# Two products of four units drawn forward, their five others in interleaved pairs, in place of one unit of eight products (Griffin-style decoder block, one Trainium2 core)

## The chip, the core and the metric

The kernel is one program on one core of a Trainium2 chip. The metric is device time in microseconds, as the median of several runs. Five engines matter, each with its own queue, which it works off in the order in which the kernel was written: TensorE (PE, with its weight loads PEld), VectorE (DVE), ScalarE (ACT), GpSimd (POOL) and SyncE (SP, which here only issues DMAs). Where one engine needs another's result it waits at that place, with everything behind it in its queue.

## The reference, cut to what matters

```python
h = rms_norm(x, norm_g)                          # x: 1 x 2048 x 1024, float32
u = jnp.einsum('bsd,dc->bsc', h, w_in)           # 1024 -> 8704 columns
v_c, b_c, c_c, z_c, q, k, v, z_a, gate_logits = jnp.split(u, SPLIT_POINTS, axis=-1)
y_c = b_c * causal_depthwise_conv(c_c * v_c, conv_w)
y_c = y_c * jax.nn.silu(z_c)
y_a = jnp.einsum('bsc,cd->bsd', y_c, w_conv_out)
q = rms_norm(q.reshape(b, s, 16, 64), q_norm_g)
k = rms_norm(k.reshape(b, s, 4, 64), k_norm_g)
o = sliding_window_attention(q, k, v, sinks) * jax.nn.silu(z_a)     # window 128
y_b = jnp.einsum('bsc,cd->bsd', o, w_attn_out)
g_a, g_b = jnp.split(jax.nn.sigmoid(gate_logits + gate_b), 2, axis=-1)
out = x + jnp.einsum('bsd,de->bse', g_a * y_a + g_b * y_b, w_out)
```

All that the change touches is in the second line: the columns q (1024 of them, in four units of 256, `q` 0 to 3) and the first half of the gate logits (`ga`, four units of 256).

## The kernel before

**Tiles and units.** The 2048 positions are two tiles of 1024. In a tile, the work of PE comes in units: 256 columns of a weight matrix, over the tile's 1024 positions, with all 1024 channels of h in the sum. A unit is a 2 x 2 x 2 block product (two halves of the columns, of the positions, and two interleaved halves of the channels). It is done with seven block products in place of eight, as Strassen and Winograd do, on sums and differences of the blocks. A product is 12 matmuls of 128x128 by 128x512: four pieces of the sum, each with a high part by a high part, high by low and low by high, since float32 values are split in two parts of a shorter format. The high part is a cast on ACT, the low part a difference on DVE (`split`, L305; `two` in `pieces_of`).

**Operands.** Products are numbered. Products 1 and 2 use plain blocks of weights and of h; 5, 6, 7 and 3 use sums of weight blocks, 5, 6, 7 and 4 sums of blocks of h. `form` makes the slices of an operand, four for each number: a cast and a difference. Operand 8 is a fourth plain block of h, which only a unit of eight plain products needs. When each norm, sum and form of tile 0 is put into the queues is a list written by hand, `OPEN_AT` (L62): entries 30 to 33 are the slices of operand 8, 70 to 73 those of operand 3.

**Steps.** The order of the whole program is set by `run` (L888). It takes a generator, a unit, which emits one product and whatever reads it (`fin`) at each yield. After each such step, counted in `tick`, `run` emits: loads of weights that there is room for; the high part of the next weight piece, if `piece` (L592) allows one; the work put down for this step in `at`, of which usually three entries stand ahead of the piece's low part; and up to four pending small DVE steps (`Woven`, L240). Keys and values are steps 1 to 16. `OPEN_AT`, `KV_PLACES` (keys) and `STEPS_0` (the steps at which the 32 attention blocks of tile 0 begin) are numbers of steps.

**Weight pieces.** `open_prep` (L578) opens the pieces of one unit at a time, and only when the unit before it has begun. A piece also needs room among eight weight buffers (`WRING`) and its raw weights, of which two units' fit. For an ordinary unit ("S") the pieces are: plain pair, single, sums, and two pairs of sums. A unit of kind "P" has only two plain pairs.

**The opening of tile 0, in order.** After keys and values come `ga` 0 as a unit of eight plain products (`qunit`, L740: two products to a bank, operands 1 and 2, then 8 and 3; steps 17 to 24), then `q` 0, 1, 2 and 3 as `sunit` (L650), seven steps each (from 25, 32, 39 and 46), then `cv` 0 from 53 and the other units. `ga` 1 to 3 come much later, ahead of `gb`. `sunit` has the order 1, 5, 6, 2, 7, 3, 4: product 1's bank is copied by ACT to the accumulator Y, 6, 7 and 4 go on in Y, 2 goes on in the bank of product 1, and 3 in that of 5 after DVE has added to it.

**PSUM.** Banks: two for products (`bank`), one Y, one pair for attention scores, and three small ones (`mbank`) for transposes, attention results, and the second units of interleaved pairs. `fin_q` (L1031) of `q` 0 and 1 copies a result by ACT, scales it into a high and a low part, stores it, and some steps later turns it with four transposes on PE in a small bank, squares it on ACT and reduces it on DVE. `fin_g` (L1411) applies tanh on ACT. `KV.back` (L976) turns the keys in a small bank (two of these fall on step 36) and splits them.

**Interleaved pairs** existed before the change elsewhere (`spair`, L694): two units' products alternate, the second unit with banks of its own.

Of the kernel before, what the change touches and what calls it, by code (L numbers as in the profile page):

```python
# [8 lines left out]
F32 = mybir.dt.float32  # L9
# [6 lines left out]
P = 128  # L16
# [3 lines left out]
H = 512  # L20
# [3 lines left out]
NKV = 4  # L24
# [29 lines left out]
PE_TURNS = ((0, 0), (0, 1))  # L54
TURN_WAIT = 3

EARLY = (1, 0)

K_AT = (1, 1, 4)

T0_SHIFT = 1
OPEN_AT = (2, 2, 2, 7, 7, 8, 5, 4, 5, 6, 4, 6, 5, 5, 6, 7, 9, 6, 7, 8, 7, 8, 8, 10, 12, 11, 14, 14, 14, 13, 17, 14, 14, 19, 18, 14, 16, 20, 20, 19, 20, 20, 18, 16, 19, 14, 20, 19, 22, 22, 23, 22, 23, 23, 8, 8, 14, 14, 26, 18, 22, 25, 27, 20, 26, 27, 21, 19, 23, 24, 18, 19, 19, 19, 28, 22, 28, 27)  # L62
KV_PLACES = (8, 11, 22, 26, 8, 11, 13, 40, 13, 31, 31, 30, 36, 36)
TURNED_AT = (6, 12)

# [12 lines left out]
WO_AHEAD = 3  # L78
THS_AT = 10
HOLD = 10  # L80
STEPS_0 = (60, 63, 71, 74, 78, 85, 92, 95, 99, 104, 110, 115, 121, 128, 131, 136, 139, 142, 146, 149, 152, 155, 159, 162, 165, 170, 173, 176, 181, 184, 187, 192)
# [44 lines left out]
def block_kernel(  # L126
# [281 lines left out]
    def load_half(i=None):  # L408

        if i is None:
            i = next(k for k in range(2 * len(plan)) if k not in raws)
        n, h = divmod(i, 2)
        kind, srcs, key = plan[n]
        if kind == "L":
            raws[i] = None
            return
        if n not in raw_of:  # L420
            raw_of[n] = rawpool.tile(
                [P, 2, 2, H], F32, tag="raw", name="w" + "_".join(str(i) for i in key) + "_raw")
        both = raw_of[n]
        if kind == "R":
            raw = both[:, h]
            for p in range(2):
                nc.sync.dma_start(raw[:, p], srcs[(2 * h + p) * P : (2 * h + p + 1) * P])

                for c in FIRST_X.get((i, p), ()):
                    xt_load(c, 0)  # L430
        elif kind in "SP":
# [12 lines left out]
        raws[i] = raw  # L444
        rawlive[0] += 1
# [11 lines left out]
    def pieces_of(n):  # L457
# [37 lines left out]
        if kind in "SP":  # L495
            def pair(h, m1, m2, nm):
                hi, lo = (v.rearrange("p (i j c) -> p i j c", i=2, c=P) for v in wpair(f"{name}_{nm}"))
                for i, m in enumerate((m1, m2)):
# [2 lines left out]
                return two(hi, lo, raw[:, h] if summed else raw[:, :, h])  # L501

            summed = []

            if kind == "P":
                return w, [(2, 2 * h, lambda h=h: pair(h, (h, 0), (h, 1), f"p{h}")) for h in range(2)]

            def single():
                hl = wpool.tile([P, 2, KP, P], F32R, tag="w", name=f"{name}_d")
# [38 lines left out]
            def second():  # L548
# [3 lines left out]
                for i, m in enumerate((7, 3)):  # L552
# [25 lines left out]
    def open_prep():  # L578
# [3 lines left out]
        if n in paired:  # L582
            both = [pieces_of(n + e) for e in range(2)]
            ready.extend(w for w, _ in both)
            todo.extend((n + e, i) + both[e][1][i] for e, i in (PAIR_LOADS if plan[n][0] == "L" else PAIR_PIECES))
            return True
        w, pieces = pieces_of(n)
        ready.append(w)
# [3 lines left out]
    def piece():  # L592
# [3 lines left out]
        n, i, cost, last, f = todo[0]  # L596
        if tick[0] < held.get(n, 0):
            return None
        need = [2 * n + i] if plan[n][0] in "TP" else [2 * n, 2 * n + 1][: 1 + min(i, 1)]
# [30 lines left out]

    B_AT = {(0, 0): 1, (1, 0): 2, (0, 1): 8, (1, 1): 3}

    def product(ps, u, n, ops, start):
        force(u, n)
        hi, lo = ready[u][n]
        for j in range(KP):
            b = ops[n][j]
            for i, (w, m) in enumerate(((hi, 0), (hi, 1), (lo, 0))):
                nc.tensor.matmul(  # L639
                    ps, lhsT=w[:, j, :], rhs=b[:, m, :],  # L640
                    start=start and j == 0 and i == 0, stop=j == KP - 1 and i == 2,
                    skip_group_check=not start)
        d = done.setdefault(u, set())
        d.add(n)
        live[0] -= sum(c for m, c in USES if n in m and m <= d)
# [91 lines left out]
        at_ = {n: 2 * order.index(n) + 2 for n in order}  # L737
        return sorted([(at_[2], (0, 0)), (at_[7], (1, 1)), (at_[3], (0, 1)), (at_[4], (1, 0))])

    def qunit(key, ops, fin):  # L740


        u = unit(key)
        nm = "_".join(str(i) for i in key)
        for q in range(2):
            for i in range(2):
                ps = bank(f"Q{nm}_{i}_{q}")
                for p in range(2):
                    force(u, (i, p))
                    hi, lo = ready[u][i, p]  # L750
                    for j in range(KP):
                        b = ops[B_AT[p, q]][j]
                        for k, (w, m) in enumerate(((hi, 0), (hi, 1), (lo, 0))):
                            nc.tensor.matmul(
                                ps, lhsT=w[:, j, :], rhs=b[:, m, :],
                                start=p == 0 and j == 0 and k == 0, stop=p == 1 and j == KP - 1 and k == 2)
                    if p:
                        fin(i, q, ps)
                        live[0] -= 2 * q
                    yield  # L760

    def kv_by_token(places, banks):

# [868 lines left out]
    for t in range(NT):  # L1632
# [9 lines left out]
        else:  # L1642
            at_(("k", t))
            at_(("v", t))
        for j in range(EARLY[t]):
            at_(("ga", t, j))
        for j in range(NKV):
            at_(("q", t, j))
        if t == 0:
            plan[2] = ("P",) + plan[2][1:]  # L1650
        for k in range(KC):
            at_(("cv", t, k))
            if k % 2:
# [302 lines left out]
    for t in range(NT):  # L1956
# [12 lines left out]
        firsts = [(("ga", t, j), fin_g(t, 0, j)) for j in range(EARLY[t])]  # L1969
        firsts += [(("q", t, j), fin_q(t, j)) for j in range(NKV)]  # L1970
        for n, (key, fin) in enumerate(firsts):
            run((qunit if t == n == 0 else sunit)(key, ops, fin))
        for k in range(KC):
            run(sunit(("cv", t, k), ops, fin_cv(t, k, ys)))
            if k % 2:
# [175 lines left out]
```

## Time and profile before

| | us |
|---|---|
| runs, median of 3 | 1903.63 |
| lowest, highest | 1900.15, 1904.28 |
| profiled execution, its own time | 1900.26 |
| its span, first to last instruction | 1898.5 |
| PE busy in the span | 1887.7 (99%) |
| DVE busy | 1499.4 (79%) |
| ACT busy | 989.8 (52%) |
| POOL busy | 607.3 (32%) |
| granted clock of TensorE | 1.00 |

A line of the timeline reads: start in us, length in us, engine, line of the kernel, operation, out<-in, shapes, count, and in brackets the idle time ahead of it with what ended it. Lengths of PE lines are modelled and overlap; the distance from one start to the next is the better measure of a matmul. All DVE work goes through one helper, so its lines bear L275 and are told apart by their tiles: `oph<-xt,oph` is the low part of an operand's slice, `xt<-xt` a sum of blocks of h, `wq_al`, `wq_sl`, `wq_tl`, `wq_d` low parts of query weights, `wq_raw` sums of them, `q_l` and `k_l` low parts of queries and keys.

### The profile page before, as it was taken

How to read it: one execution, taken by the hardware profiler on the slowest of the kernel's cores; microseconds unless marked ns; L12 is line 12 of the kernel's file. 1: busy time of each engine (PE TensorE's matmuls, PEld its weight loads, DVE VectorE, ACT ScalarE, POOL GpSimd, SP SyncE). 2: the span in 40 equal slices, each digit the busy share in tenths (PEclk: the TensorE clock that was granted, in tenths of full speed). 3: DMA queues.
4: the chain of work that ended last, by engine and by line, in shares of the span. 5: the costliest groups of instructions: out<-in, count | busy, mean ns of one | idle time of the engine just before them, and what ended most of it. 6: DMA issues, size and time to landing. Idle time of an engine off the chain costs nothing.

```text
span 1898.5 us, 27267 instructions
## 1 busy us (share of the span) xinstructions
PE 1887.7 (99%) x8670; PEld 1572.5 (83%) x8670; DVE 1499.4 (79%) x2364; ACT 989.8 (52%) x1967; POOL 607.3 (32%) x846
## 2 busy tenths in 40 slices
PE   9999999999999999999999999999999999999999
PEld 7888888888887888888888888888888888888887
DVE  7988898887777767668799788887878877787654
ACT  7665455456666443434565455556666434444321
POOL 2083435335655000011372344445655000121000
PEclk9999999999999999999999999999999999999999
DMA  8296555568777857895584654567778977779653
GB/s 295 80 244 172 164 166 171 163 189 250 238 231 222 305 196 244 283 280 120 157 232 128 183 173 155 167 206 228 240 242 267 304 279 262 278 198 264 212 175 110
DMA packets 222495, 402.20 MB, mean 212 GB/s; under 512 B 30032, under 2 KB 104784, under 8 KB 212880
## 3 DMA queue, kind: packets, MB, share of 16 engines
q1 hardware_dynamic: 188224, 313.10, 50.6%
q0 software_dynamic: 30528, 78.94, 15.8%
q10 hardware_dynamic: 3600, 8.42, 1.3%
q8 instruction: 69, 1.13, 0.2%
q14 instruction: 74, 0.61, 0.1%
HBM read 271.09 MB, written 129.25 MB: 211 GB/s over the span
## 4 chain that ended last, share of the span: by engine, by line
PE 67%; DMA 1%; ACT 0%; issue 0%; DVE 0%; POOL 0%; DVEq 0%; POOLq 0%; ACTq 0%; SPq 0%
PE Y L639 24%; PE ya L1479 5%; PE Vcv L639 2%; PE Xcv L639 2%; PE Xyb L639 2%; PE Vo L639 2%; PE Xo L639 2%; PE Vyb L639 2%; PE Vza L639 2%; PE Xza L639 2%; PE Vz L639 2%; PE Xz L639 1%; PE po L1338 1%; PE Vga L639 1%; PE Xgb L639 1%; PE Vb L639 1%
## 5 line engine op out<-in xcount | busy, mean ns | idle before, releaser
L1300 POOL DMA_DIRECT2D x<-fd x256 | 139.5, 551 | 124.3 <-DMA fd<-f 48.9
L1274 ACT ACTIVATE p<-s,st,rq 128x129 f32<-128x129 f32 x256 | 114.2, 457 | 33.0 <-DVE st L275 21.2
L1321 POOL TENSOR_SCALAR_AFFINE_SELECT xh<-xh 64x512 fp32r<-64x512 f32 x64 | 61.5, 961 | 153.5 <-DVE xl L275 101.1
L1293 POOL DMA_DIRECT2D fd<-f x64 | 36.9, 576 | 196.7 <-DVE f L275 173.0
L1562 POOL DMA_DIRECT2D mt<-tha x16 | 13.8, 861 | 255.0 <-DVE tha L275 228.1
L639 PE MATMUL Xcv<-oph,wcv_ah 128*128 128x512 f32 x256 | 78.9, 389 | 0.0
L1321 POOL TENSOR_SCALAR_AFFINE_SELECT yp<-xl 64x512 fp32r<-64x512 f32 x64 | 70.8, 1106 | 3.1
L1321 POOL TENSOR_SCALAR_AFFINE_SELECT xl<-xl 64x512 fp32r<-64x512 f32 x64 | 68.6, 1072 | 4.4
L1321 POOL TENSOR_SCALAR_AFFINE_SELECT yp<-yp 64x512 fp32r<-64x512 f32 x64 | 57.6, 899 | 4.2
L275 DVE TENSOR_TENSOR o<-po,o 64x256 f32<-64x256 f32 x128 | 53.5, 418 | 4.8 <-ACT o L1350 3.8
L275 DVE SCALAR_TENSOR_TENSOR y<-u,cols,y 128x512 f32<-128x512 f32 x64 | 53.6, 837 | 3.7 <-ACT y L1387 2.5
L639 PEld LDWEIGHTS Xcv<-oph,wcv_ah 128*128 128x128 f32 x256 | 47.7, 188 | 9.4
L275 DVE TENSOR_TENSOR p<-p,st 128x512 f32<-128x512 f32 x64 | 50.3, 786 | 3.4
L275 DVE STREAM_TRANSPOSE f<-p 128x512 f32<-128x512 f32 x64 | 45.5, 711 | 8.6 <-DMA fd<-f 5.7
L466 ACT CAST wcv_sh<-wcv_raw 128x1024 fp32r<-128x1024 f32 x16 | 16.8, 1051 | 67.0 <-DVE wcv_raw L275 67.0
L1274 ACT ACTIVATION_READ_ACCUMULATOR p<-s,st,rq 128x1 f32 x256 | 51.2, 200 | 0.0
L1249 PEld LDWEIGHTS s<-kq,q 128*128 128x128 f32 x256 | 46.1, 189 | 5.8 <-ACT s L1237 1.9
L1350 ACT COPY o<-po 64x256 f32<-64x256 f32 x128 | 47.1, 368 | 6.4 <-DMA wpd_yb<-wph_yb 3.2
L639 PE MATMUL Xcv<-oph,wcv_al 128*128 128x512 f32 x128 | 49.9, 390 | 0.0
L1078 POOL DMA_DIRECT2D q2d<-q_l x64 | 44.1, 688 | 17.8 <-DMA q2d<-q_h 4.9
L2052 POOL DMA_DIRECT2D oc<-ocd x12 | 6.5, 543 | 134.9 <-ACT ophc L306 128.7
L1078 POOL DMA_DIRECT2D q2d<-q_h x64 | 44.2, 690 | 17.2 <-ACT q_h L1073 7.9
(711 smaller groups left out, 6408.2 us busy)
## 6 DMA issues: line engine op xcount, KB each, us to landing
gd<-th SPq DMA_DIRECT2D x64, 256.0 KB, 2.8
wcv_raw<-in_w_units SPq DMA_DIRECT2D x16, 1024.0 KB, 5.5
q<-q2d SPq DMA_DIRECT2D x64, 256.0 KB, 5.4
v<-vd SPq DMA_DIRECT2D x128, 128.0 KB, 3.6
fd<-f POOLq DMA_DIRECT2D x64, 256.0 KB, 4.3
x<-fd POOLq DMA_DIRECT2D x256, 64.0 KB, 3.6
th<-gd SPq DMA_DIRECT2D x48, 256.0 KB, 5.0
wga_raw<-in_w_units SPq DMA_DIRECT2D x8, 1024.0 KB, 5.3
```

What stands on the lines that cost most here:

```text
L275: r = f(*args, **kw)
L466: return (lambda: nc.scalar.copy(hi, src), lambda: vec.tensor_tensor(out=lo, in0=src, in1=hi.bitcast(F32), op=ALU.subtract))
L639: nc.tensor.matmul(ps, lhsT=w[:, j, :], rhs=b[:, m, :], start=start and j == 0 and i == 0, stop=j == KP - 1 and i == 2, skip_group_check=n ...
L1078: nc.gpsimd.dma_start(q2d[t][j][half, q * 2 * HB : (q + 1) * 2 * HB, i, e, :], src[HALVES[e]].bitcast(F32).rearrange("p (b x) -> p b x", x ...
L1249: nc.tensor.matmul(sp[:, h, c, skip : 3 * HD], lhsT=q2[:, h, c, :], rhs=kq[:, 0, keys], start=c == 0, stop=False)
L1274: nc.scalar.activation(out=p[:, i, :], in_=sg[:, i, HD : 3 * HD + 1], func=AF.Exp, bias=st[:, 1, i : i + 1], scale=rv[:, i // 2, i % 2 : i ...
L1293: nc.gpsimd.dma_start(fd, f)
L1300: nc.gpsimd.dma_start(x[QUADS[k]], src[k])
L1321: nc.gpsimd.affine_select(out=d4, in_=s4, pattern=[[0, 2], [-32 * sg, 2], [0, G], [-sg, 32]], compare_op=ALU.is_gt if prev else ALU.is_ge, ...
L1338: nc.tensor.matmul(po[:, cs], lhsT=v2[:, kind + h, :], rhs=xx[:, :, h * HD : (h + 1) * HD], start=n == h == 0, stop=n == 2 and h == 1)
L1350: nc.scalar.copy(ov, pov[oth, :, e])
L1479: nc.tensor.matmul(ps, lhsT=w[:, j, cs], rhs=o[:, m, :], start=n == 0 and i == 0, stop=n == KC - 1 and i == 2)
```

## The change

The unit of eight products (`qunit`, kind "P") is gone, and with it operand 8. `q` 0, `ga` 0, `q` 1 and `ga` 1 are now each cut in two. First come the *heads*: products 1 and 2 of `q` 0, `ga` 0, `q` 1, `ga` 1, in that order (`hpair`; steps 17 to 24). Both go into one bank; between them ACT copies product 1 to a tile of its own, `heads`. Then come the *rests*, in two interleaved pairs (`rpair`): products 5, 6, 7, 3, 4 of `q` 0 and `ga` 0 by turns (steps 25 to 34), then of `q` 1 and `ga` 1 (35 to 44). With product 5, ACT copies the kept head into Y, for the second unit into a small bank that it holds for nine steps. `q` 2 begins at step 45, and what follows `ga` 1's old place is one step earlier than before.

The heads have a kind of weight unit "F" (half of each unit's raw weights, two plain pieces), the rests a kind "M" (the whole raw weights once more, and the pieces sums, pair, pair, single, by turns for the two units; the next unit's pieces are held back five steps). The slices of operand 3 move from steps 18 and 19 to 26 to 28. `STEPS_0` begins six steps earlier; its later entries are one or two steps earlier.

```diff
-EARLY = (1, 0)
+EARLY = (2, 0)
-OPEN_AT = (... 23, 24, 18, 19, 19, 19, 28, 22, 28, 27)
+OPEN_AT = (... 23, 24, 26, 27, 28, 28, 28, 22, 28, 27)
-STEPS_0 = (60, 63, 71, 74, 78, 85, 92, 95, 99, ... 181, 184, 187, 192)
+STEPS_0 = (54, 59, 66, 69, 77, 80, 84, 91, 98, ... 179, 182, 185, 190)
+REST = (5, 6, 7, 3, 4)
+REST_PIECES = tuple((e, i) for i in range(4) for e in range(2))
+REST_HOLD = 5
...
+        elif kind == "F":
+            raw = both[:, h].rearrange("p k (j c) -> p k j c", c=P)
+            src = w_units[unit_index(srcs[h])].rearrange("r (k h x) -> r k h x", k=2, h=2)[:, :, 0]
+            nc.sync.dma_start(both[:, h], src)
...
+            if kind == "M":
+                return w, [(0, 0, sums_first), (2, 0, first), (2, 0, second), (1, 2, single)]
...
-    def qunit(key, ops, fin):
+    def hpair(key, ops, subs):
         u = unit(key)
+        for e, (sub, fin) in enumerate(subs):
+            xb = bank(f"X{nm}")
+            product(xb, u, 1, ops, True, (e, 1))
+            heads[sub] = slot([P, H], F32, f"head{nm}")
+            nc.scalar.copy(heads[sub], xb)
+            yield
+            product(xb, u, 2, ops, False, (e, 2))
+            fin(0, 0, xb)
+            yield
+    def rpair(keys, ops, fins):
+        us = [unit(key) for key in keys]
+        held[us[1] + 1] = tick[0] + REST_HOLD
+        vb, yb, s5 = [None, None], [Y, None], [None, None]
+        for n, e in ((n, e) for n in REST for e in range(2)):
+            u, fin, nm = us[e], fins[e], nms[e]
+            if n == 5:
+                vb[e] = bank(f"V{nm}")
+                product(vb[e], u, 5, ops, True)
+                s5[e] = spare(f"s5{nm}")
+                nc.scalar.copy(s5[e], vb[e])
+                if e:
+                    yb[e] = mbank(f"Y{nm}").rearrange("p b q -> p (b q)")
+                nc.scalar.copy(yb[e], heads.pop(keys[e]))
+            elif n == 6:
+                product(yb[e], u, 6, ops, False)
+                add(vb[e], s5[e], yb[e])
...
-    put(OPEN_AT[30], lambda: form(0, 8, 0, st))
-    put(OPEN_AT[31], lambda: form(0, 8, 1, st))
-    put(OPEN_AT[32], lambda: form(0, 8, 2, st))
-    put(OPEN_AT[33], lambda: form(0, 8, 3, st))
...
+        if t == 0:
+            subs = [[(("q", 0, j), fin_q(0, j)), (("ga", 0, j), fin_g(0, 0, j))] for j in range(2)]
+            for j in range(2):
+                run(hpair(("f", j), ops, subs[j]))
+            for j in range(2):
+                run(rpair([k for k, _ in subs[j]], ops, [f for _, f in subs[j]]))
+        for j in range(2 if t == 0 else 0, NKV):
+            run(sunit(("q", t, j), ops, fin_q(t, j)))
```

More of the change, by code (lines that the diff above doesn't have):

```diff
@@ L493, in pieces_of, with head @@
                        for i, ms in enumerate(((1, 2), (6, 5), (3, 7), (4,)))]
-        if kind in "SP":
+        if kind == "F":
+            def head(e):
+                hi, lo = (v.rearrange("p (i j c) -> p i j c", i=2, c=P) for v in wpair(f"{name}_{e}"))
+                for i in range(2):
+                    w[e, 1 + i] = (hi[:, i], lo[:, i])
+                return two(hi, lo, raws[2 * n + e])
+            return w, [(2, 1, lambda e=e: head(e)) for e in range(2)]
+        if kind in "SM":
             def pair(h, m1, m2, nm):
@@ L584, in open_prep @@
             ready.extend(w for w, _ in both)
-            todo.extend((n + e, i) + both[e][1][i] for e, i in (PAIR_LOADS if plan[n][0] == "L" else PAIR_PIECES))
+            order = {"L": PAIR_LOADS, "M": REST_PIECES}.get(plan[n][0], PAIR_PIECES)
+            todo.extend((n + e, i) + both[e][1][i] for e, i in order)
             return True
@@ L738, in pair_outs @@
         return sorted([(at_[2], (0, 0)), (at_[7], (1, 1)), (at_[3], (0, 1)), (at_[4], (1, 0))])
-    def qunit(key, ops, fin):
+    heads = {}
+    def hpair(key, ops, subs):
         u = unit(key)
[L744 to L760, printed above, removed]
+        for e, (sub, fin) in enumerate(subs):
+            nm = "_".join(str(i) for i in sub)
+            xb = bank(f"X{nm}")
[6 more added lines that the diff above has]
+            yield
@@ new lines, in rpair @@
+    def rpair(keys, ops, fins):
+        us = [unit(key) for key in keys]
+        held[us[1] + 1] = tick[0] + REST_HOLD
+        nms = ["_".join(str(i) for i in key) for key in keys]
+        vb, yb, s5 = [None, None], [Y, None], [None, None]
[12 more added lines that the diff above has]
+                add(vb[e], s5[e], yb[e])
+            elif n == 7:
+                product(yb[e], u, 7, ops, False)
+                fin(1, 1, (yb[e], s5[e]))
+            elif n == 3:
+                product(vb[e], u, 3, ops, False)
+                fin(0, 1, vb[e])
+            else:
+                product(yb[e], u, 4, ops, False)
+                fin(1, 0, yb[e])
+            yield
```

41 lines of the change are left out of this document (21 added, 20 removed).

## The prediction

> **What bounds the kernel now.** I read the page first, then the list of waits of TensorE (PE), then busy time by stage for the stretch that the change touches.
>
> ```profile
> span 1898.5 us, 27267 instructions
> PE 1887.7 (99%) x8670; PEld 1572.5 (83%) x8670; DVE 1499.4 (79%) x2364; ACT 989.8 (52%) x1967; POOL 607.3 (32%) x846
> ...
> PE po L1338 <- POOL yp L1321: 1.7, 2, 1.1
> PE po L1338 <- POOL xl L1321: 1.5, 2, 1.2
> PE s L1249 <- ACT s L1237: 1.4, 1, 1.4
> ...
> core 0: us, PE busy (x) PEld busy (x) DVE busy (x) ACT busy (x) POOL busy (x), PEclk, DMA share, GB/s
> 52.00:74.00 22.00, 21.93 (x97) 17.82 (x96) 22.00 (x34) 13.76 (x24) 0.00 (x0) 1.00 0.10 38
> 74.00:91.00 17.00, 17.00 (x78) 14.07 (x77) 16.69 (x27) 10.86 (x20) 0.00 (x0) 1.00 0.21 78
> 91.00:105.00 14.00, 14.00 (x74) 11.70 (x73) 11.98 (x21) 11.84 (x19) 8.52 (x14) 1.00 0.73 187
> 105.00:137.00 32.00, 32.00 (x154) 26.69 (x153) 27.53 (x66) 16.57 (x28) 25.02 (x39) 1.00 0.91 252
> ```
>
> PE is the bound nearly everywhere: its largest waits on other engines add up to under 5 us of 1898.5. So a product taken away is worth its full PE time, and a wait put into PE's queue costs its full length, because no slack follows that could absorb it. The stages show the second fact: from 52 to 91 us, where the unit of eight products and the first query unit run, VectorE (DVE) is busy 38.69 of 39 us at the same time. PE does not wait there, but DVE has nothing to spare. That is exactly the stretch that is rearranged.
>
> **The product that goes.**
>
> ```profile
> 647.34 2.72 PE Xza L639 x12
> 52.20 0.63 PE L754 MATMUL Qga<-oph,wga_p0h 128*128 128x512 f32 x2
> ```
>
> The chain of waits gives 2.72 us for twelve matmuls, one product. Step 17, the first after the keys and values, starts at 52.20. Two query and two gate units cost 8+7+7+7 = 29 products before and 28 after. PE loses one product: -2.7 us. The four slices of operand 8 go with it; they lie on ScalarE (ACT) and DVE.
>
> **Four copies between two products of one bank.** In a head, product 2 accumulates into the PSUM bank that ACT must first copy to the head's tile. In the old unit of seven, another bank's product stood between the two. PE's queue is in order, so everything behind waits too. The price comes from two places where ACT had nothing else to do:
>
> ```profile
> 649.67 0.39 PE L639 MATMUL Xza<-oph,wza_al 128*128 128x512 f32 x1
> 649.90 0.62 PE L639 MATMUL Vza<-oph,wza_sh 128*128 128x512 f32 x2
> 650.15 0.57 ACT L657 COPY Y<-Xza 128x512 f32<-128x512 f32 x1 [0.72 <-PE Xza L639]
> ...
> 588.61 0.17 ACT L1237 COPY s<-sinks 128x4 f32<-128x4 f32 x1
> 588.83 0.47 PE L1249 MATMUL s<-kq,q 128*128 128x192 f32 x2 [1.44 <-ACT s L1237]
> ...
> 90.68 0.60 PE L980 MATMUL pbk<-ident,k_n 128*128 128x128 f32 x4
> 91.03 2.99 PE L639 MATMUL Y<-oph,wq_d 128*128 128x512 f32 x12
> ...
> L1417 ACT ACTIVATE th<-Qga,hbias 128x512 f32<-128x512 f32 x4 | 2.7, 685 | 3.4 <-PE Qga L754 3.4
> L306 ACT CAST oph<-xt 128x512 fp32r<-128x512 f32 x18 | 10.3, 617 | 5.2 <-DVE xt L275 4.7 <-DVE oph L275 0.4
> L466 ACT CAST wq_ah<-wq_raw 128x1024 fp32r<-128x1024 f32 x4 | 4.2, 1044 | 0.0
> L1073 ACT ACTIVATE q_h<-q_t,gqk 128x512 fp32r<-128x512 f32 x16 | 11.6, 722 | 0.5 <-ACT q_t L790 0.3
> ```
>
> The last matmul of a product starts at 649.67; the next would start at 649.90. The copy starts at 650.15 and takes 0.57, and PE follows an ACT copy by 0.05 (588.78 to 588.83). So PE would go on at 650.77: 0.87 us lost per head with an idle ACT. In the third and fourth head ACT comes late: ahead of the third copy stand a tanh (0.69), four casts (0.62 each) and a scaling (0.72), over 3 us even where they overlap, for a product of 2.72. But four transposes of the first query results lie between the two products and cover 0.35 (90.68 to 91.03). I take 4 x 0.93 = +3.7 us; the ends are 1.9 (0.4 covered in each) and 6 (ACT 0.6 later in each).
>
> **DVE's queue up to product 7.**
>
> ```profile
> 55.44 0.74 DVE L275 SCALAR_TENSOR_TENSOR xt<-xt,cols,rb 128x512 f32<-128x512 f32 x1
> 56.10 0.68 DVE L275 TENSOR_TENSOR oph<-xt,oph 128x512 fp32r<-128x512 f32 x1
> 56.70 1.22 DVE L275 TENSOR_TENSOR wq_al<-wq_raw,wq_ah 128x1024 fp32r<-128x1024 f32 x1
> 57.84 0.69 DVE L275 TENSOR_TENSOR xt<-xt 128x512 f32<-128x512 f32 x1
> ...
> 83.99 1.29 DVE L275 TENSOR_TENSOR oph<-xt,oph 128x512 fp32r<-128x512 f32 x2 [0.28 <-ACT oph L306]
> ...
> 85.23 0.62 PE L639 MATMUL Y<-oph,wq_th 128*128 128x512 f32 x2
> ```
>
> Back to back, DVE takes 0.60 for a 512-wide difference (56.10 to 56.70), 1.14 for a 1024-wide one and 0.66 for a scaled one. Before, DVE runs from operand 8's first slice (56.10) without a break, but for 0.28, to operand 7's first slice (84.68), and the product that reads it starts at 85.23: half a microsecond of slack. After the change this product stands on the same step, 29. The list of DVE work up to that slice changes so:
> - in: low parts of two heads 2 x 1.14, and for q0 and ga0 together eight single sums 8 x 0.60 and four low parts 4 x 1.14: 11.6;
> - out: q0's pieces, 4 x 1.14 + 3 x 0.60 = 6.4;
> - in: for the query heads, now six or more steps earlier, two scaled low parts 2 x 0.66 and two reductions 2 x 0.60: 2.5;
> - out: two slices of operand 8 (1.2), and three of operand 3 that now come later (1.8).
>
> That is +4.7. Two more slices of operand 8 stood ahead of 56.10, so DVE starts at 54.9. It also idles where it never did: ACT's casts now stand in its queue behind copies that wait for PE. The first head's cast cannot end before 52.20 + 2.72 + 0.25 (lag) + 1.5 (copy 0.57, cast 1.04, less their overlap) = 56.7: 1.8 idle. Followed the same way I get 0.5 at step 18, 1.2 at 19, 0.6 at 20, 1.5 at 22 (the query's low part behind copy and scaling of product 22), and 1.7 at 25 and 26 (casts that wait for sums, low parts that wait for casts): 7.3. Operand 7's first slice is then done at 54.9 + 28.3 + 4.7 + 7.3 = 95.2. PE would be there at 52.2 + 12 x 2.72 + 0.7 (transposes) + 3.7 = 89.2. The six of lateness show as waits of the products of steps 25, 26 and 29, and step 30 waits for its own sum behind it, about 0.6 more: +6.6 us. The ends are 2 (idle half as long, ledger two less) and 9.
>
> **The bank at step 36.**
>
> ```profile
> 109.81 1.03 PE L980 MATMUL pbk<-ident,k_n 128*128 128x128 f32 x8
> 110.45 1.08 ACT L306 CAST k_h<-pbk 128x512 fp32r<-128x512 f32 x2 [1.30 <-PE pbk L980]
> 110.68 0.60 PE L913 MATMUL ptq<-ident,q_t 128*128 128x128 f32 x4
> 111.14 1.28 DVE L275 TENSOR_TENSOR k_l<-pbk,k_h 128x512 fp32r<-128x512 f32 x2
> ...
> DVE q_l L275 <- ACT q_h L1073: 4.3, 4, 2.1
> ```
>
> Before, step 36 takes three of the three small PSUM banks: two for the keys' transposes, one for a query's. After, the second pair's other gate accumulator takes one at the same step, so a transpose must wait until DVE has read a bank. With DVE on time that is k_l's first end, 111.8, against 110.68: 1.2 us. But DVE will be late. Steps 31 to 35 give it 16.4 us (two units' sums and low parts alone 9.4) for 15 us of PE, where it had 4.3 us of waits to spare before (91 to 137), and the casts again alternate with the sums. Followed through, it is 7 to 8 us behind there. I take 6, nearer to that end: +6.0, between 1.2 and 8.
>
> ACT also changes table twice more, because tanh of the gates now surrounds the keys' square root:
>
> ```profile
> 96.59 1.28 ACT L296 ACT_TABLE_LOAD   x1
> 97.88 0.21 ACT L296 ACTIVATE k_t<-k_ms 128x16 f32<-128x16 f32 x1
> ```
>
> 2 x 1.28, and this is in the lateness just told. The Trainium skill ("ScalarE: Activation LUTs", What ACT_TABLE_LOAD costs) puts a switch at 1283 ns plus a drain of about 1380 ns; this trace agrees with the first, and the square root begins 0.01 us behind the load, so I count no drain. By the page the two switches would delay ACT by 2.8 us more, and the forecast would be up to that much longer.
>
> **What hides.** Half of each of four units is loaded once more, 2 MB on SP's queue:
>
> ```profile
> wcv_raw<-in_w_units SPq DMA_DIRECT2D x16, 1024.0 KB, 5.5
> ```
>
> 5.5 us for 1 MB, with the DMA engines at 0.10 from 52 to 74 us. The heads are loaded where two whole units were, the rests a pair ahead; cost nothing, at most 5.5 if the second pair's load came late. Gate unit 1 only moves. Attention starts six steps earlier by number but, with the lateness above, at nearly the same microsecond. Its end moves one step against the z units, where the three waits first shown partly lie: between -3 and +3; I take 0.
>
> **Sum:** -2.7 + 3.7 + 6.6 + 6.0 = +13.6. The profiled execution before took 1900.26 us, so 1913.9. Its runs have a median of 1903.63 (1900.15 to 1904.28), so the profiled one lies at their fast end; I add half of that distance: **1915.5 us**.
>
> **The rivals.**
> - *DVE catches up; only the copies cost.* If the idles are short and the bank wait stays at its lower end: -2.7 + 3.7 + 1.2 = +2.2, about 1904 to 1906. For it: DVE loses 5 us of operand work ahead of step 25. Against: half a microsecond of slack at 85.23. Chance 0.19 (within 0.2%, which is about what a measurement of this kernel can tell from no change, 3.8 us).
> - *In between:* the queue term as forecast, the bank wait 1.2 to 3: about 1908 to 1911. Chance 0.20.
> - *Faster: the copies are covered.* It takes ACT's copy to end inside other PE work. It decides where the transposes of step 21 and 23 and the keys' work fill the gap, and then DVE, relieved of operand 8, is early: -2.7, with attention's 3 us of waits gone as well 1895 to 1900. Against: at steps 17 and 19 nothing of PE's stands between the two products. Chance 0.07.
> - *The clock falls.* All zero-products of the start run at half speed:
>
> ```profile
> 1.52 4.45 PE L1701 MATMUL Y<-zero 128*128 128x512 f32 x10 [1.52 <-DVE zero L197]
> ```
>
> 0.43 us each against 0.227 (649.67 to 649.90). If a wait of 6 us brings that back for as long as at the start, ten matmuls, it costs 10 x 0.2 = 2 us more: 1917.5. Before, no wait is longer than 1.4 and the granted clock is 1.00 in every stage, so no row can show it. Chance 0.09. The Trainium skill ("TensorE: Matmul & The Clock Gate", Part 1) has a rule of this kind, with an idle window of about 3.4 us after which the clock is halved; no run here shows it so far.
>
> **The numbers.** The forecast has 0.45. The range, 1902 to 1923, leaves out the faster case and the far ends of the bank and clock. Faster by over 0.2%: 0.07. Within: 0.19. Slower by over 0.2%: 0.74.
>
> **What would show it.** Right: four waits of PE on ACT at the heads, 0.8 to 1.1 us each; waits of PE on DVE at steps 25, 26, 29 and 30 of about 6 us together; one of several microseconds at the transposes of step 36; DVE's idle time on ACT between 52 and 91 us near 7 instead of 0.3; PE at 28 products where there were 29. Wrong: PE without waits from 75 to 100 us, or DVE idle under 3 us there.

## The result, and the profile after

| | before | after |
|---|---|---|
| median, us | 1903.95 (4 runs) | 1923.37 (4 runs) |
| lowest, highest | 1900.15, 1905.34 | 1920.15, 1924.70 |
| ratio, 95% interval | | 1.0104 (1.0092 to 1.0116) |
| profiled execution, its span | 1900.26, 1898.5 | 1920.15, 1918.4 |

The kernel became 19.4 us slower, where 13.6 more than the profiled execution, 1915.5 in all, was forecast. It lies 0.4 us above the range. First the page's head of the kernel after, then its busy time by stage, in the columns of the prediction's stages.

```profile
span 1918.4 us, 27206 instructions
...
PE 1892.1 (99%) x8658; PEld 1570.6 (82%) x8658; DVE 1509.1 (79%) x2371; ACT 990.0 (52%) x1969; POOL 609.5 (32%) x846
```

```profile
52.00:74.00 22.00, 19.88 (x87) 15.59 (x86) 16.59 (x25) 11.75 (x19) 2.91 (x5) 1.00 0.30 84
74.00:91.00 17.00, 14.54 (x64) 10.93 (x62) 16.27 (x25) 10.73 (x18) 2.58 (x4) 1.00 0.20 47
91.00:105.00 14.00, 10.45 (x46) 7.80 (x45) 13.05 (x21) 8.65 (x17) 1.26 (x3) 1.00 0.35 125
105.00:137.00 32.00, 25.03 (x114) 20.14 (x113) 18.64 (x30) 17.95 (x27) 16.40 (x26) 0.89 0.73 202
...
152.00:318.00 166.00, 162.55 (x752) 134.37 (x751) 148.65 (x257) 89.55 (x196) 78.85 (x109) 1.00 0.60 173
...
560.00:640.00 80.00, 79.74 (x380) 66.82 (x379) 63.49 (x91) 54.21 (x115) 43.94 (x58) 1.00 0.75 235
```

Before, PE was busy in every microsecond from 74 to 318. Now it is idle for 2.1, 2.5, 3.6 and 7.0 us in the first four stages, and the granted clock, 1.00 in all stages before, is 0.89 in the fourth. DVE, which had not a tenth of a microsecond to spare from 52 to 74, is idle for 5.4 there. PE also loses 3.5 us in the units that follow (152 to 318). At the end of tile 0's attention it gains, against this row of before:

```profile
560.00:640.00 80.00, 77.17 (x362) 64.05 (x361) 60.96 (x91) 50.74 (x96) 35.67 (x44) 1.00 0.77 248
```

The list of PE's waits in the kernel after, from 52 to 152 us, has the tile that waited, the tile waited for, the total, how often and the longest:

```profile
PE pbk L1025 <- ACT k_h L309: 6.2, 1, 6.2
PE Y L657 <- DVE Vq L278: 2.7, 1, 2.7
PE Xga L657 <- ACT headga L771: 1.5, 2, 0.8
PE Xq L657 <- ACT headq L771: 1.4, 2, 0.8
PE Vga L657 <- DVE wga_sl L278: 1.4, 2, 1.1
PE Yga L657 <- DVE Vga L278: 0.8, 1, 0.8
PE ptq L958 <- DVE k_l L278: 0.6, 1, 0.6
PE Vq L657 <- DVE wq_sl L278: 0.4, 1, 0.4
```

Every wait that the prediction named is there: four at the heads (`Xq`, `Xga` on the copies), four at steps 25, 26, 29 and 30 (`Vq`, `Vga`, `Y`, `Yga` on DVE), one of several microseconds at the keys' transposes (`pbk`). A wait's price is a little more than its entry, as lengths of PE lines overlap; by the distances from start to start, less the usual 0.227 us, the heads cost 3.9 us, steps 25 to 30 5.9, step 35 0.4, and the bank 7.3.

Why the bank comes so late is seen in the timelines of ACT (first) and DVE (second):

```profile
107.08 1.28 ACT L299 ACT_TABLE_LOAD   x1
...
108.61 1.28 ACT L1462 ACT_TABLE_LOAD   x1
...
115.96 1.05 ACT L473 CAST wga_sh<-wga_raw 128x1024 fp32r<-128x1024 f32 x1 [2.82 <-DVE wga_raw L278]
...
120.76 1.04 ACT L473 CAST wq_th<-wq_raw 128x1024 fp32r<-128x1024 f32 x1 [2.56 <-DVE wq_raw L278]
```

```profile
112.17 1.23 DVE L278 TENSOR_TENSOR wq_sl<-wq_raw,wq_sh 128x1024 fp32r<-128x1024 f32 x1 [2.67 <-ACT wq_sh L473]
...
117.04 1.23 DVE L278 TENSOR_TENSOR wga_sl<-wga_raw,wga_sh 128x1024 fp32r<-128x1024 f32 x1 [1.11 <-ACT wga_sh L473]
...
121.84 1.23 DVE L278 TENSOR_TENSOR wq_tl<-wq_raw,wq_th 128x1024 fp32r<-128x1024 f32 x1 [1.11 <-ACT wq_th L473]
...
126.67 0.68 DVE L278 TENSOR_REDUCE qss<-ptq 128x8 f32<-128x512 f32 x1
```

Neither engine is busy all the time from 105 to 137 us (DVE 18.6 and ACT 18.0 of 32), yet both are late: ACT's cast waits for DVE's sum, DVE's low part for ACT's cast, and the next sum stands behind that low part. Each queue is in order, so whatever stands in it waits along. DVE's `qss`, which reads a query's transposes and so frees their bank, ends at 127.35; PE starts its transpose at 127.50. The list of waits names ACT's `k_h`, which ends 0.1 us after `qss`; but `k_h` reads the group of transposes before, and that bank is free only when DVE's `k_l` has read it too, at 129.1. In the run r1 below the same wait is put down to `qss`.

Then PE runs slowly for a while. The distance between two starts of 128x512 matmuls was 0.227 us before; it is 0.43 from 130.5 to 131.3, and 0.23 again from 131.9:

```profile
127.50 1.09 PE L1025 MATMUL pbk<-ident,k_n 128*128 128x128 f32 x4 [6.18 <-ACT k_h L309]
129.15 1.12 PE L958 MATMUL ptq<-ident,q_t 128*128 128x128 f32 x4 [0.55 <-DVE k_l L278]
129.92 1.20 PE L657 MATMUL Y<-oph,wq_sh 128*128 128x512 f32 x2
130.92 0.63 PE L657 MATMUL Y<-oph,wq_sl 128*128 128x512 f32 x1
131.34 0.74 PE L657 MATMUL Y<-oph,wq_sh 128*128 128x512 f32 x2
131.93 0.39 PE L657 MATMUL Y<-oph,wq_sl 128*128 128x512 f32 x1
```

That costs 1.0 us here. The four runs have mean granted clocks of 0.998, 0.997, 0.996 and 0.997 at 1920.15, 1922.43, 1924.70 and 1924.31 us. A thousandth of mean clock is at most 1.9 us lost at half speed (3.8 us of 1918 at half the clock), and less where PE waits meanwhile, as here. So more such stretches can explain up to 1.9 of the 3.2 us by which the profiled run lies below the median.

### The profile page after: what moved, and what is told of

Its sections match the earlier page's. It is cut to its first block, busy times and chain, and to the rows that moved or that the text cites. A ratio compares the mean times of both kernels' runs of the same rounds, so it can differ in the third digit from the quotient of the medians.

```text
span 1918.4 us, 27206 instructions
## 1 busy us (share of the span) xinstructions
PE 1892.1 (99%) x8658; PEld 1570.6 (82%) x8658; DVE 1509.1 (79%) x2371; ACT 990.0 (52%) x1969; POOL 609.5 (32%) x846
## 4 chain that ended last, share of the span: by engine, by line
PE 71%; DMA 1%; DVE 1%; SPq 0%; ACT 0%; issue 0%; POOL 0%; DVEq 0%; ACTq 0%; POOLq 0%
PE Y L657 26%; PE ya L1524 4%; PE Xcv L657 2%; PE Vcv L657 2%; PE Xyb L657 2%; PE Vo L657 2%; PE Xo L657 2%; PE Vyb L657 2%; PE Vza L657 2%; PE Xza L657 2%; PE Xgb L657 2%; PE Vgb L657 2%; PE Vz L657 2%; PE Xz L657 2%; PE po L1383 2%; PE Vga L657 1%
```

## The experiments

Two theories were put against each other. **L**: all waits from step 25 on are one lateness (of DVE, as I then thought); what is taken away at one place comes back at the next. **S**: each wait costs its own length. The table has PE's idle time by stage (length less busy time), the granted clock in the second and third, and the ratio to the kernel before. What the stages hold shifts by up to 30 us between kernels; the waits compared stay inside them.

| | 52-74 | 74-105 | 105-140 | 152-318 | 560-640 | clock | ratio (95%) |
|---|---|---|---|---|---|---|---|
| before | 0.1 | 0 | 0 | 0 | 2.8 | 1.00, 1.00 | 1 |
| after | 2.1 | 6.0 | 7.0 | 3.5 | 0.3 | 1.00, 0.90 | 1.0104 (1.0092 to 1.0116) |
| e1 | 0 | 5.1 | 7.0 | 3.5 | 0 | 0.94, 0.85 | 1.0089 (1.0074 to 1.0105) |
| e2 | 2.1 | 5.2 | 2.8 | 3.5 | 0 | 0.94, 1.00 | 1.0067 (1.0053 to 1.0081) |
| r4 | 2.1 | 5.2 | 0 | 4.1 | 0 | 0.94, 1.00 | 1.0054 (1.0037 to 1.0071) |
| r1 | 2.1 | 2.8 | 2.1 | 3.5 | 0.3 | 1.00, 1.00 | 1.0059 (1.0044 to 1.0074) |
| p1 | 2.1 | 6.7 | 10.4 | 3.5 | 0 | 0.89, 0.86 | 1.0147 (1.0132 to 1.0162) |
| e3 | 2.1 | 5.2 | 6.9 | 1.1 | 1.9 | 0.94, 0.90 | 1.0114 (1.0100 to 1.0128) |
| p2 | 0.1 | 0 | 0 | 0.3 | 1.1 | 1.00, 1.00 | 0.9990 (0.9980 to 1.0000) |
| e4 | 0.4 | 0 | 0 | 0 | 0 | 1.00, 1.00 | 0.9984 (0.9975 to 0.9992) |
| p3 | 0 | 8.3 | 6.8 | 1.1 | 0 | 0.83, 0.90 | 1.0108 (1.0093 to 1.0123) |
| r2 | 0 | 5.8 | 0 | 1.9 | 0 | 1.00, 1.00 | 1.0037 (1.0022 to 1.0052) |
| r3 | 0 | 3.3 | 0 | 1.9 | 0 | 1.00, 1.00 | 1.0010 (1.0001 to 1.0019) |

**e1, the heads by turns** (after, in `hpair`):

```diff
         for e, (sub, fin) in enumerate(subs):
-            xb = bank(f"X{nm}")
-            product(xb, u, 1, ops, True, (e, 1))
-            nc.scalar.copy(heads[sub], xb)
-            yield
-            product(xb, u, 2, ops, False, (e, 2))
+            xbs.append(bank(f"X{nm}"))
+            product(xbs[e], u, 1, ops, True, (e, 1))
+            nc.scalar.copy(heads[sub], xbs[e])
+            yield
+        for e, (sub, fin) in enumerate(subs):
+            product(xbs[e], u, 2, ops, False, (e, 2))
```

> The kernel after, with the two heads of a pair by turns: product 1 of q, product 1 of ga, product 2 of q, product 2 of ga, so that ACT's copy of one head lies beside the other's product. In the profile after, the four head copies hold PE for 3.9 us together. Theory L (one lateness: DVE is late, and a wait that is taken away ahead of it comes back at the next product that waits for DVE): the head waits go, but the waits of steps 25, 26, 29 and 30 grow from 5.9 to 8 or 9, the wait for the bank at step 36 stays at 6 to 6.5; together 3 to 4 us less than after would be wrong by the theory's letter, 0 to 1 less if every microsecond comes back; followed through the queues I get 3.5 less, since the copies also end 2 to 4 us earlier and ACT's casts behind them: about 1920. Theory S (separate waits: each costs its own length): 3.9 less and the waits at 25 to 30 unchanged at 5.9, about 1919.5. The two are told apart by the waits at steps 25 to 30, not by the time.

1919.35 us; by the ratios 0.0015 x 1902 = 2.9 us less than after, though the two intervals overlap. All four head waits are gone. The waits of steps 25 to 30 went from 0.5, 1.3, 2.9, 0.3 and 1.0 to 1.4, 1.9, 2.3, 0.3 and 0.2, the last one covered by 1.6 us lost to half-speed matmuls. In r2, which has the same heads and no half speed, it stays at 1.0, and they add up to 6.7 against 5.9. So the copies were worth most of their 3.9 us by themselves; about a fifth came back as lateness. Theory L in its strict form fails here.

**e2, the keys' second half later** (after):

```diff
-KV_PLACES = (8, 11, 22, 26, 8, 11, 13, 40, 13, 31, 31, 30, 36, 36)
+KV_PLACES = (8, 11, 22, 26, 8, 11, 13, 40, 13, 31, 31, 30, 46, 47)
```

> The kernel after, with the second half of the keys' transposes (two entries of KV_PLACES) moved from step 36 to steps 46 and 47, where the second pair has given back its small bank. In the profile after, the wait for this bank is 6.3 + 0.9 us and is followed by about nine matmuls at half speed (1.7 us). Theory L: the bank's wait goes, but DVE is as late as before, so that 3 us or so appear at products of steps 37 and 38 that read what DVE makes; no wait is longer than 3.5 us, the clock stays at 1.00 throughout, and the run is 4 (waits) + 1.7 (clock) = about 6 us shorter than after: 1917.5. Theory S: the whole wait and the clock go, 7.2 + 1.7 = 9 shorter: 1914.5. If the clock were not the wait's doing, PEclk would still show a dip in the windows behind 105 us.

1914.78 us, 0.0037 or 7.0 us less than after, between the two. PE's waits from 105 to 140 us:

```profile
PE Y L657 <- ACT Y L792: 2.0, 1, 2.0
PE Yga L657 <- ACT Yga L792: 0.6, 1, 0.6
PE Vga L657 <- DVE wga_sl L278: 0.2, 1, 0.2
```

The bank's 7.3 us are gone and 2.9 (2.1 and 0.8 from start to start) came back, at the places that L named, but on ACT's copies of the heads to the accumulators, not on DVE. The clock there is back at 1.00: the half speed had been the long wait's doing. (From 74 to 105 us, which the edit does not touch, e2 has half speed and after has none; p4 below explains it.)

**r4, the keys' norm later too** (e2, and `KV_PLACES`' tenth entry 44 in place of 31).

> The kernel after with the keys' second half at steps 46 and 47 (as in e2) and its norm, with the square root between two tanh and so two table loads of ACT (2 x 1.28 us), at step 44 in place of 31. In e2 2.1 and 0.8 us of waits came up at steps 37 and 38 in place of the bank's 6.3. If the table loads and the norm's small steps put ACT and DVE behind there: these waits go, 3 us shorter than e2, ratio 1.005. If it is DVE's backlog from steps 25 to 30 alone: within 1 us of e2, ratio 1.0065.

1913.74 us, 0.0013 less than e2; in time the two cannot be told apart. But the profile answers: PE waits nowhere from 105 to 140 us. So the norm with its two table loads had put the queues behind at steps 31 to 38, and not a backlog from steps 25 to 30. The loads and the norm's small steps moved together, so their shares are not separated.

**p1, weight sums on POOL** (after, in `sums_first` and `more` for the four interleaved units):

```diff
-  vec.chain(*added(n), lambda: sub(raw[:, 0, 0], raw[:, 0, 1], raw[:, 0, 0]))
+  add(raw[:, 0, 1], raw[:, 0, 1], raw[:, 1, 1], nc.gpsimd)
+  sub(raw[:, 0, 0], raw[:, 0, 1], raw[:, 0, 0], nc.gpsimd)
...
+  sub(raw[:, 0, 1], raw[:, 1, 1], raw[:, 0, 0], nc.gpsimd)
+  sub(raw[:, 1, 0], raw[:, 1, 0], raw[:, 0, 0], nc.gpsimd)
```

> The kernel after, with the 16 sums of the four interleaved units' weights done by POOL in place of DVE, at the same places in the order. DVE loses 8 x 0.60 us in steps 21 to 26 and as much again in 31 to 36. POOL has no row for such a sum; its nearest, selects on 64x512, take 0.9 to 1.1 us, and POOL is nearly idle there (2.9 of 22 us from 52 to 74). Theory L (one lateness of DVE's queue): both the waits of steps 25 to 30 and the bank's fall by about what DVE is relieved of: 5.9 to about 3 and 6.3 to 1.2, no half-speed matmuls behind the bank: 9 us of waits in the opening where after has 18.7, and 1.7 of clock less: 10 to 11 us shorter than after, about 1912. Theory A (ACT's queue holds it up: casts behind copies that wait for PE): the waits stay, 0 to 2 us shorter, 1921 to 1923. If POOL's sums slow DVE down while they run, DVE's times of 0.60 and 1.14 would show it.

1929.30 us: not 10 us less but 8 more (0.0043). A sum of POOL's, and one group of DVE's (first the kernel after from 74 to 105 us, then p1 from 72 to 94; count, busy time, mean ns):

```profile
72.76 1.29 POOL L313 TENSOR_TENSOR wq_raw<-wq_raw 128x512 f32<-128x512 f32 x1
```

```profile
L278 DVE TENSOR_TENSOR xt<-xt,xt 128x512 f32<-128x512 f32 x5 | 3.3, 685 | 0.0
```

```profile
L278 DVE TENSOR_TENSOR xt<-xt,xt 128x512 f32<-128x512 f32 x4 | 5.4, 1358 | 0.0
```

While POOL adds, DVE's sums take twice as long, 1.36 us in place of 0.69. So DVE was not relieved. The Trainium skill ("SBUF — State Buffer", SBUF: two separate sides) says that a DVE operation with two inputs in SBUF and a POOL operation that reads SBUF exclude each other through a shared port; the rows agree. Slowing the pair of queues raised the waits for operands and bank (13.0 to 17.1 us idle from 74 to 140).

**r1, the sums left out** (after, without those 16 sums at all).

> The kernel after without the 16 weight sums of the four interleaved units: their products use the weight blocks as they were loaded, so part of the computation is left out. What p1 could not show, as POOL's sums held DVE up (0.60 us became 1.2 to 1.8 while POOL worked): DVE is relieved of 8 x 0.60 us in steps 21 to 26 and as much in 31 to 36, and nothing is put in their place. Theory L (DVE's queue): waits of steps 25 to 30 from 5.9 to about 3, the bank's from 6.3 to about 1.2, the half speed behind it gone: 9 us of waits and 1 to 1.7 of clock less than after, about 1912 to 1913, ratio 1.005. Theory A (ACT's casts stand behind copies that wait for PE, and DVE only follows): within 2 us of after, ratio 1.010.

1913.20 us, 0.0045 or 8.6 us less than after. PE's waits from 74 to 140 us are now:

```profile
PE pbk L1030 <- DVE qss L278: 1.1, 1, 1.1
PE ptq L963 <- DVE k_l L278: 1.0, 1, 1.0
PE Xga L662 <- ACT headga L776: 0.8, 1, 0.8
PE Yga L662 <- DVE Vga L278: 0.8, 1, 0.8
PE Vga L662 <- DVE wga_sl L278: 0.6, 1, 0.6
PE Y L662 <- DVE Vq L278: 0.4, 1, 0.4
```

Steps 25 to 30 fell from 5.9 to 2.5 and the bank from 7.3 to 2.4, and the clock is 1.00 throughout. The sums were what ACT's casts waited for (2.82 and 2.56 in the rows above): with them gone, ACT waits for DVE only 1.8 us from 74 to 128 (12.5 in after), while DVE waits for ACT as much as it did (12.5, against 11.4). That is theory L, with both engines in place of DVE alone; the norm of r4 holds up the same chain on its other side. r1 takes load off DVE and a link out of the chain at once and cannot tell them apart. From 74 to 105 us DVE is busy 29.3 of 31 us in after, so there its load may be enough by itself; for the bank, where it idles 13 of 32, the chain is the better reading.

**e3 and p2, attention's start.** e3 is after with `STEPS_0` of the kernel before, each entry less one (59, 62, 70, ... 191); p2 is before with `STEPS_0` of after, each plus one (55, 60, 67, ... 191).

> The kernel after, with the attention blocks of tile 0 at the steps of the kernel before, each one earlier, as all that follows the gate units moved by one: attention begins at step 59 instead of 54, and its end is nearly unchanged against after. In the profile after, the stage of the cv units (152 to 318 us) has 4.9 us of waits of PE, mostly for DVE, where before it had none. Theory A: these come from attention's earlier start, which lies over the work on queries 2 and 3: they fall under 1.5 us, and the time is 3 to 4 us shorter than after (1919.5 to 1920.5), less what comes back at the end of attention. Theory Q: they come from queries 2 and 3 themselves, which are six steps later than before: the waits stay at 4 to 5 us, and the time is that of after, 1922 to 1925. At the end of tile 0's attention (about 578 to 638 us) the waits stay under 1 us if what counts there is one step against the z units; they come back to 3.7 if it is the list's other differences.

> The kernel before, with tile 0's attention at the steps of the kernel after (each one later, as the gate unit that moved is one step; its last ten are those of the kernel before moved one earlier). It tells where the 4.9 us of waits in the cv units come from, of which 1.9 stay when after gets the old steps. Overlap of attention's first blocks with the late queries 2 and 3: before, these queries are done six steps earlier, so under 1.5 us of waits between 150 and 320 us and 0 to 2 us less than before for the end (1900 to 1902). The early start by itself: 3 to 5 us of waits, about 1904.

e3 takes 1923.25 us, its ratio that of after: 2.3 us less idle from 152 to 318, 1.6 more at attention's end. p2 has 0.3 us in the first place, though attention starts early there. So neither half makes all the waits alone. Here are the first 40 us of the `cv` units, counted from the first matmul of `cv` 0, in before, p2, e3 and after (DVE's busy time is the third figure behind the stage's length):

```profile
156.00:196.00 40.00, 40.00 (x183) 33.32 (x183) 37.79 (x86) 21.87 (x49) 10.26 (x16) 1.00 0.50 141
...
155.80:195.80 40.00, 39.70 (x180) 32.74 (x180) 38.60 (x88) 22.75 (x52) 13.10 (x21) 1.00 0.67 187
...
193.30:233.30 40.00, 38.86 (x177) 31.46 (x176) 38.47 (x88) 21.69 (x53) 15.04 (x23) 1.00 0.58 163
...
193.20:233.20 40.00, 36.92 (x170) 29.99 (x170) 38.70 (x86) 23.57 (x57) 17.12 (x26) 1.00 0.59 164
```

DVE has been full there all along, 37.8 of 40 us before and 38.5 to 38.7 in the other three. What differs is where attention begins: its first score matmul starts 24 us behind the start of `cv` 0 before (180.5), 11 behind in p2 (166.7), 5 behind in e3 (198.7) and 9 ahead of it in after (184.0). PE's idle time from 152 to 318 rises in the same order: 0, 0.3, 1.1, 3.5. So these waits come from attention's first blocks, moved forward into the work on queries 2 and 3 and the first `cv` units. The old step numbers of e3 bring back only part of the old order, as the queries and `cv` units themselves moved six steps. No run put the first blocks as far behind `cv` 0 as before.

**e4, attention's end** (before, the last ten entries of `STEPS_0` one less: 158, 161, 164, ... 191).

> The kernel before, with only the last ten attention blocks of tile 0 one step earlier. Before, PE waits 3.7 us between 560 and 620 us, after only 0.5 at the same place, where I took 0 for attention's end. If that is the one step against the z units: the waits go, 3 us less than before, 1900.9 (ratio 0.9984). If it is chance or something else of the change (attention's start, the heads' work): no difference, ratio 1.000 within 0.0005.

1899.72 us, ratio 0.9984: about 3 us faster than the kernel before, as expected. PE's waits from 560 to 640 us are gone (2.8 before). So the gain of after at this place is the one step against the z units, and has nothing to do with heads and rests. p2, with the same end, keeps 1.1 us and reaches 0.9990.

**p3, r2 and r3, the waits removed together.** p3 is e1, e2 and p1 with attention's first 22 blocks at the steps of e3 and its last ten as in after. r2 is p3 with the sums back on DVE and the norm at step 44 as in r4. r3 is r2 without the sums.

> The kernel after with all that the runs so far point to: heads by turns, the keys' second half at steps 46 and 47, the 16 weight sums on POOL, attention's first 22 blocks at the old steps and its last ten as in after. Theory L: about 4.4 us of waits left in the opening (steps 25, 26, 29, 30), 2 in the cv units, none at attention's end, no half-speed matmuls: against before -2.7 + 4.4 + 2 - 3 = +0.7, so 1902 to 1904, ratio 1.000 to 1.001; no gain over the kernel before even so. Theory S (each wait by itself): 5.9 + 0.4 of waits in the opening and the rest the same: ratio about 1.002. If what is left were below 3 us it would be the faster kernel of the two.

> The kernel after with heads by turns, the keys' second half at steps 46 and 47, its norm at step 44 in place of 31, attention's first 22 blocks at the old steps and its last ten as in after; the weight sums on DVE as in after. Theory L: waits in the opening of about 7 (steps 25, 26, 29, 30), up to 1.6 of half speed, 2 in the cv units, none at attention's end: against before -2.7 + 7.1 + 1 + 2 - 3 = +4.4, ratio 1.002 to 1.003. If the removals did not add up, the ratio would stay at e2's 1.0067 or above 1.005.

> The one before with the 16 weight sums left out as well (part of the computation is left out). A bound on what the change could bring with DVE relieved: about 4.4 us of waits left in the opening, no half speed; -2.7 + 4.4 + 2 - 3 = +0.7, ratio 1.000. If DVE were all of it, the waits would go too and the ratio fall to 0.998.

p3 misses by 0.010: PE is idle for 15.1 us from 74 to 140, against 5.8 in r2, without POOL's sums and with the norm later. r2 has 1909.61 us, two thirds of the loss undone: no wait from 105 to 140, none at attention's end, but 5.8 us at steps 25 to 30 and 1.9 behind. r2's ratio, 1.0037, is a little above the 1.002 to 1.003 of theory L. r3 has 1905.56, ratio 1.0010, so the sums are not all of it. Even so the order with one product less is not faster than before, let alone than e4.

**p4, the clock by itself** (before, with 14 waits put in):

```diff
+            pt = mbank(f"hold{tick[0]}")
+            nc.tensor.transpose(pt[:, 0, :], ident, ident)
+            nc.scalar.copy(probe, pt[:, 0, :32])
+            for _ in range(n):
+                nc.scalar.copy(probe, probe)
+            nc.tensor.transpose(pt[:32, 1, :], probe, ident)
```

> The kernel before with 14 waits of PE put in at quiet places (eight in the first conv branch at 800 to 900 us, six between the last units): PE turns a small tile, ACT copies it n times onto itself (4 to 26 copies of 128x32), and PE turns the result. It computes the same output, later. Rule of a whole idle window (the Trainium skill, TensorE: Matmul & The Clock Gate, Part 1: about 3.4 us): waits under 3.4 us cost their own length alone, longer ones are followed by about ten matmuls at 0.43 us in place of 0.227, +2 us. Theory of a share of busy time: the half speed comes from 2 to 2.5 us on already, as behind the 2.3 and 2.9 us waits at 90 us in three of the kernels run, and not each time for one length; its price is 1.4 to 1.8 us whatever the wait's length.

It ran once (1974.37 us), and only its trace is used. Of the 14 waits, the five shorter ones (1.27 to 2.27 us) are followed by no half speed, the seven longer ones (3.32 to 6.82) all are. Between them are two of the same length, one without and one with half speed behind it. Here are both (in brackets) in the timeline of PE, and then the stretches of 3.41 us that they fall into, with PE's busy time behind the length and PEclk as the last figure but two:

```profile
909.29 0.28 PE L1501 MATMUL hold<-ident,probe 128*32 128x128 f32 x1 [2.83 <-ACT probe L1500]
...
1870.86 0.40 PE L1501 MATMUL hold<-ident,probe 128*32 128x128 f32 x1 [2.83 <-ACT probe L1500]
```

```profile
904.72:908.13 3.41, 1.75 (x9) 1.15 (x7) 3.41 (x5) 1.38 (x7) 0.14 (x1) 1.00 0.41 114
908.13:911.54 3.41, 2.25 (x11) 1.89 (x12) 3.38 (x7) 2.18 (x8) 0.71 (x1) 1.00 0.70 130
...
1867.28:1870.69 3.41, 0.75 (x4) 0.33 (x2) 2.70 (x3) 2.63 (x12) 0.00 (x0) 1.00 0.42 156
1870.69:1874.10 3.41, 3.24 (x9) 2.57 (x10) 0.00 (x0) 0.11 (x1) 0.00 (x0) 0.50 0.79 226
```

These stretches are the clock's own. The clock of this trace is 0.50 from 836.45 to 839.86, 853.51 to 856.93, 870.58 to 877.41, 891.06 to 897.89 and 1870.69 to 1874.10, among others: each lasts 3.41 us or twice that, and their starts lie whole multiples of 3.41 us apart. The clock thus goes by windows of 3.41 us. The first wait is split by the border at 908.13 and leaves 1.66 us idle in its emptier window; the second lies almost whole in one and leaves 2.66 idle, and the next window runs at half speed. The traces of the other kernels agree: in after the wait ahead of 95 us leaves at most 1.75 us idle in a window, in e2 the same wait leaves 2.53, and only e2 has half speed behind it. The price is 1.3 to 1.6 us where one window is at half speed and 2.4 to 2.8 where two are.

## Why the prediction was off

By distances from start to start, profile against profile (1920.15 less 1900.26 is 19.9 us), the sum reads:

| step of the prediction | forecast | measured |
|---|---|---|
| the product that goes | -2.7 | -2.7 |
| four head copies | +3.7 | +3.9 |
| DVE's queue up to product 7 | +6.6 | +5.9 |
| the bank at step 36 | +6.0 | +7.3 (and 0.4 at step 35) |
| the clock | 0 (a rival, +2) | +1.0 |
| attention: 152 to 318, 318 to 560, 560 to 640 us | 0 | +4.9, +0.7 and -2.9 |
| gaps under 0.06 us, the very end | | +1.4 |

Of the 6.3 us between 13.6 and 19.9, attention makes 2.7, the bank and step 35 1.7, the small gaps 1.4 and the clock 1.0; the copies add 0.2, and the queue takes 0.7 away. The product is worth what was said: 29 became 28. The copies and the queue were right in place and size; DVE's idle time on ACT up to 95 us is 6.7 us against the 7.3 that was added up.

The step that failed is the last term: "Attention starts six steps earlier by number but, with the lateness above, at nearly the same microsecond. Its end moves one step against the z units ... I take 0." Its two halves are different things. The end was worth -2.9, which e4 shows to be the one step. For the start the microsecond was right (first score matmul at 184.0, before at 180.5), but it is the wrong measure: queries 2 and 3 and the `cv` units start 37 us later (`cv` 0 at 193.2, before at 156.0), so attention's first blocks now come ahead of `cv` 0 and among the work on the queries. DVE had little to spare there before, too (busy for 37.8 of 40 us). This stage, without any wait before, was never costed, and gave +4.9 (1.9 in e3, 0.6 in p2). That +4.9 and -2.9 partly cancel is luck.

Two more terms were taken too small. For the bank the working had "7 to 8 us behind" and took 6, for no reason but its lower end; 7.3 came. Its mechanism was half right: with DVE idle for 13 of 32 us it is not so much DVE's load that makes it late as ACT and DVE waiting for each other, and the keys' norm with the two table loads, called "in the lateness just told", was a cause of its own (r4: 2.8 us). The clock's fall was given 0.09 and belongs to the forecast itself, as soon as that forecast contains a wait of 6 us: p4 found half speed behind every wait from 3.3 us on. The Trainium skill's rule that the prediction weighed ("TensorE: Matmul & The Clock Gate", Part 1) was the better guide here. The rival's size, 2 us for ten matmuls, was twice what came: of 6.8 us at half speed PE waited for 3.3.

Last, half of the distance to the median was added, 1.7 us; the profiled run of after lay 3.2 below its median. By the clocks of the four runs up to 1.9 of that can be stretches at half speed. The prediction's list of PE's largest waits also leaves out one of 1.5 us at the very start (`Y` on `zero`), which is in both kernels and changes nothing.

What is not settled: the 1.9 us idle from 152 to 318 in r2 are 1.1 for DVE's `Vcv` and 0.8 for ACT's `s`, but no run removes them; and the 4.2 us that stay at steps 25 to 30 in r3, with the sums gone (2.5 in r1), were not taken apart.

## What to carry over

Where two in-order engines hand each other halves of every operand (cast, difference, sum, cast), cost the chain through both and not the busier one's load: here both were idle for over 13 of 32 us and late all the same, and leaving out 16 short sums brought 8.6 us. When units change places, list what every later unit's side work now lies on, in steps and not by the clock, and look at the busy share of the engine it needs in that stage, even where nothing waits yet. A wait of PE of 3.3 us or more is to be priced with 1.3 to 2.8 us of half-speed matmuls behind it, less what the wait itself takes up of the half-speed time; one of 2 to 3 us may bring it too.

## What the hardware showed

- The half speed needs no long pause. 2.83 us of waiting brought it once in two times, 3.32 to 6.82 us seven times in seven, 1.27 to 2.27 never in five.
- In the traces of all these runs half speed comes, behind the start and up to the last matmul, in stretches of 3.41, 6.83 or 10.24 us. Each begins behind a window of 3.41 us in which PE was idle for 1.7 us or more; behind windows idle for up to 1.9 us the clock also stayed full, so the border lies about there, at half the window. After three waits of 1.4, 1.9 and 2.3 us within 17 us half speed came in e1 but not in r2, which has the same waits: 1.88 us idle in both, at the border. The Trainium skill ("TensorE: Matmul & The Clock Gate", Part 1) speaks of an idle window of about 3.4 us that runs freely; the length and the fixed grid agree, but the window need not be idle throughout.
- POOL's sums on 128x512 took 1.29 to 1.76 us and made DVE's sums, 0.69 by themselves, take 1.36 on average and up to 1.80.
